# Down projection of a SwiGLU feed-forward block: from eight products of a two-by-two block to seven, in rounds between the gate and up products, for two of three token groups

## The chip, the cores and the metric

One core of one Trainium2 chip. The metric is device time in microseconds; before the change 2132.35 us is the median of three runs (2131.14 to 2133.75).

## The reference

One layer of a hybrid decoder on 2048 prompt tokens and 8 single-token samples (2056 columns in all, model width 1024): a normed input projection, a gated linear recurrence beside sliding-window attention, an output projection with residual, and then the part that matters here, all in float32:

```
hn = rmsnorm(h, norm2_g)
ff = silu(hn @ w_gate) * (hn @ w_up)        # w_gate, w_up: 1024 x 2816
y  = h + ff @ w_down                        # w_down: 2816 x 1024
y_out = rmsnorm(y, final_norm_g)
```

## The kernel before, in words

Every matrix product is done three times over, for precision: an operand is split into a high part, rounded to the engine's 32-bit replacement type (float32r), and a low part, the remainder; three matmuls (high x high, high x low, low x high) add up in one PSUM bank. ScalarE makes the high parts, the vector engine or GpSimd subtracts to get the low parts.

The feed-forward block (from about 700 us on) works through three groups of tokens (HALVES, L34: two halves of 344, then 342 columns each). In a group it goes through the 22 chunks of 128 hidden features as 11 pairs. For each pair, gate and up are each a two-by-two block product (two hidden chunks, two token halves, two halves of the model width) done Strassen-Winograd-wise: seven products (PRODS, L35) of four 128-deep pieces each, 7 x 4 x 3 = 84 matmuls. `products` (L1043) issues them, sums them from PSUM into tiles c (L1069 to L1102), applies silu on ScalarE (L1061), multiplies up by gate on GpSimd (L1064) and splits the result into fh and fl (L1066, L1067). `down` (L1105) takes the pair's 2 x 2 tiles of ff and the two rows of w_down: for each of eight output chunks m and two token halves n it does six matmuls into a bank (L1120 to L1122), and the vector engine adds the bank to the residual y in SBUF (L1124): 96 matmuls and 16 reads per pair.

The down projection of pair p stands between the gate and the up products of pair p + 1; that of the last pair stands at the group's end, with the first three gate products of the next group ahead of it (N_EARLY).

The weights of w_gate and w_up need sums for the seven products. In the first group these are built, split and stored to DRAM (split_s, four of seven a pair, L1033); the later groups load them (L1017), L_SS = 11 us ahead of use, and split the three plain ones (L986, L987). Weights of w_down are loaded (L1039) and split in each group, their low part on GpSimd (L1041). Split weights lie in a ring of eight tiles (wp and wp2), raw ones in a ring of seven.

A ring of sixteen big tiles (bigp) holds three slots of 344 columns in each tile: eight tiles for the activations of products 1, 2 and 6 (`hn_load`), six for the residual y (`y_load`, L982), so fourteen a group; tiles are handed out in turn, and a new owner waits for the old one. `hn_mix` prepares the next group's activations while a group runs (loads L322, scaling L326 and sums L334 on the vector engine, stores L330). `finish` (L1128) does the final norm of a group and stores it (L1148, L1151), inside the next group's first pairs.

PSUM has eight banks in five pools: acc has three, s two, t, o and m one each; the products and the down tiles take them in turn (`ps_tile`).

The order of the work is written out as times: each generator yields the time in a nominal schedule (U_M = 1.76 us a product, U_D = 14.1 us a down projection) at which its next step is due, and that time is the priority with which a scheduling pass, which simulates the program, orders each engine's queue. Every engine works its queue in order. All loads and stores here are issued by the sync engine's queue.

```
T_B = [T_B0 + i * (NPAIR * U_P + D_TB) for i in range(3)]
def t_gate(gi, p):
    return T_B[gi] + (2 * U_G + (p - 1) * U_P if p else 0)
def t_down(gi, p):
    return t_gate(gi, p + 1) + U_G if p < NPAIR - 1 else ...
```

Of the kernel before, what the change touches and what calls it, by code (L numbers as in the profile page):

```python
# [42 lines left out]
T_FS = 12.0  # L43
L_SS, L_ST = 11.0, 5.0
D_TB = 0.0
# [7 lines left out]
T_H3, D_H3 = T_B0 + 38, 4.0  # L53
T_B = [T_B0 + i * (NPAIR * U_P + D_TB) for i in range(3)]
O_KF = [8, 9, 10, 11, 12, 13, 0, 4, 1, 5, 2, 6, 3, 7]
# [89 lines left out]
def hybrid_step(tc, xT, xR, vecs, cst, gatew, win, wout, wgate, wup, wdown, kT, vC, ck, cv, sconv, sh0,  # L145
# [4 lines left out]
    with ExitStack() as ctx:  # L150
# [779 lines left out]
        with ExitStack() as bctx:  # L930
# [10 lines left out]
            def turn(key, n):  # L941
                cnt[key] += 1
                return cnt[key] % n
# [16 lines left out]

            ys, ws, gss, ffs = {}, {}, {}, {}

            def t_gate(gi, p):
                return T_B[gi] + (2 * U_G + (p - 1) * U_P if p else 0)

            def t_up(gi, p):
                return t_gate(gi, p) + U_G + (U_D if p else 0)

            def t_down(gi, p):
                return t_gate(gi, p + 1) + U_G if p < NPAIR - 1 else t_up(gi, p) + U_G + (N_EARLY * U_M if gi < len(HALVES) - 1 else 0)  # L970

            def t_prod(gi, p, x, i):
                t = t_gate(gi, p) if x == "g" else t_up(gi, p)
                return t + U_M * i - (U_D if gi and not p and x == "g" and i < N_EARLY else 0)

# [18 lines left out]
            def mixed_weights(src, gi, p, x):  # L994
# [17 lines left out]
                for i, r in enumerate(PRODS):  # L1012
# [18 lines left out]
                    if r in SPLIT:  # L1031
                        with at(tr - L_ST if p else tr + 2):
                            nc.sync.dma_start(split_s[x][p, SPLIT.index(r)], w.bitcast(F32))  # L1033

            def down_weights(gi, p, t):
                for i, (q, h) in enumerate(((0, 0), (0, 1), (1, 0), (1, 1))):
                    yield t + U_D / 4 * i - 16
                    v = raw_tile(f"rd{gi}_{p}_{h}{q}")
                    nc.sync.dma_start(v, wdown[2 * p + h][:, q * 512:q * 512 + 512])  # L1039
                    yield t + U_D / 4 * i - 9  # L1040
                    keep_weights(("d", gi, p, h, q), f"d{gi}_{p}_{h}{q}", v, nc.gpsimd)  # L1041

            def products(gi, p, x):  # L1043
# [3 lines left out]
                if up:  # L1047
                    fh = {(h, n): fp.tile([P, TP], F32R, tag=f"fh{h}{n}", name=f"fh{gi}_{p}_{h}{n}")
                          for h in range(2) for n in range(2)}
                    fl = {(h, n): fp.tile([P, TP], F32R, tag=f"fl{h}{n}", name=f"fl{gi}_{p}_{h}{n}")  # L1050
                          for h in range(2) for n in range(2)}
                    ffs[gi, p] = fh, fl
# [3 lines left out]
                c11, c12, c21, c22 = (C[h, n][:, :nn] for h in range(2) for n in range(2))  # L1056

                def finished(h, n):
# [5 lines left out]
                    (nc.vector if DVE_MUL == 1 or DVE_MUL == 2 and p == NPAIR - 1 else nc.gpsimd).tensor_tensor(v, v, g, op=ALU.mult)  # L1064
                    hi, lo = fh[h, n][:, :nn], fl[h, n][:, :nn]
                    nc.scalar.copy(hi, v)  # L1066
                    nc.vector.tensor_tensor(lo, v, hi.bitcast(F32), ALU.subtract)  # L1067

# [36 lines left out]
            def down(gi, p):  # L1105
                t = t_down(gi, p)
                last = p == NPAIR - 1
                yield t, ("udone", gi, p)
                fh, fl = ffs.pop((gi, p))
                nn = HALVES[gi][0][1]  # L1110
                order = [(m, n) for n in range(2) for m in range(KD)] if last else \
                    [(m, n) for m in range(KD) for n in range(2)]
                for i, (m, n) in enumerate(order):
                    yield t + U_D * i / 16, ("d", gi, p, 0, m // 4), ("d", gi, p, 1, m // 4)
                    ps = ps_tile(f"pd{gi}_{p}_{m}_{n}")[:, :nn]
                    for h in range(2):
                        w = ws["d", gi, p, h, m // 4]
                        c = m % 4 * P
                        hi, lo = fh[h, n][:, :nn], fl[h, n][:, :nn]
                        nc.tensor.matmul(ps, w[:, 0, c:c + P], hi, start=h == 0, stop=False)  # L1120
# [50 lines left out]
            for gi in range(len(HALVES)):  # L1171
# [6 lines left out]
                for n in range(2):  # L1178
                    te = tb + NPAIR * U_P
                    ch.add(finish(gi, n, te + 6 + 8 * n, 1.0) if gi < 2 else finish(gi, n, te + U_D * (n / 2 - 1) + 1, 0.8))  # L1180
                for p in range(NPAIR):
                    ch.add(mixed_weights(wgate, gi, p, "g"))
                    ch.add(mixed_weights(wup, gi, p, "u"))
                    ch.add(down_weights(gi, p, t_down(gi, p)))
                    ch.add(products(gi, p, "g"))
                    ch.add(products(gi, p, "u"))
                    ch.add(down(gi, p))
            ch.run()
# [101 lines left out]
```

## Time and profile before

| | |
|---|---|
| median of three runs | 2132.35 us |
| the profiled execution, its own time | 2133.11 us |
| its span, first to last instruction | 2131.3 us |
| mean granted TensorE clock | 0.989 |
| TensorE busy | 2057.4 us, 97% |
| vector engine busy | 1346.7 us, 63% |
| ScalarE busy | 838.2 us, 39% |
| GpSimd busy | 863.4 us, 41% |

Times in the rows count from the span's start. PE is TensorE's matmuls, DVE the vector engine, ACT ScalarE, POOL GpSimd, SP the sync engine's queue. A matmul's row is longer than its distance to the next one, since matmuls are pipelined. L12 is line 12 of the kernel. A wait is put down to what ended it.

### The profile page before, as it was taken

How to read it: one execution, taken by the hardware profiler on the slowest of the kernel's cores; microseconds unless marked ns; L12 is line 12 of the kernel's file. 1: busy time of each engine (PE TensorE's matmuls, PEld its weight loads, DVE VectorE, ACT ScalarE, POOL GpSimd, SP SyncE). 2: the span in 40 equal slices, each digit the busy share in tenths (PEclk: the TensorE clock that was granted, in tenths of full speed). 3: DMA queues.
4: the chain of work that ended last, by engine and by line, in shares of the span. 5: the costliest groups of instructions: out<-in, count | busy, mean ns of one | idle time of the engine just before them, and what ended most of it. 6: DMA issues, size and time to landing. Idle time of an engine off the chain costs nothing.

```text
span 2131.3 us, 34656 instructions
## 1 busy us (share of the span) xinstructions
PE 2057.4 (97%) x12454; PEld 1947.2 (91%) x12454; DVE 1346.7 (63%) x2551; ACT 838.2 (39%) x1714; POOL 863.4 (41%) x748
## 2 busy tenths in 40 slices
PE   8999899999999899999999999999999999999997
PEld 8887687878877899999999999999999999999997
DVE  6767974766985857767766655555546644444445
ACT  5746773563653443333234422222224322212222
POOL 5211342020122687677666523442344433323422
PEclk9999899999999999999999999999999999999998
DMA  8764394575678866665656575656557655545442
GB/s 303 251 214 139 117 305 157 169 254 188 214 247 264 305 205 210 207 210 201 213 185 219 193 245 193 206 179 211 188 167 239 204 197 180 169 158 167 163 156 73
DMA packets 188395, 429.72 MB, mean 202 GB/s; under 512 B 23072, under 2 KB 64432, under 8 KB 188208
## 3 DMA queue, kind: packets, MB, share of 16 engines
q1 hardware_dynamic: 185024, 424.99, 59.8%
q10 hardware_dynamic: 3200, 2.51, 0.4%
q8 instruction: 99, 1.62, 0.3%
q14 instruction: 72, 0.59, 0.1%
HBM read 326.46 MB, written 102.04 MB: 201 GB/s over the span
## 4 chain that ended last, share of the span: by engine, by line
PE 74%; DVE 10%; DMA 8%; ACT 3%; issue 3%; POOL 1%; SPq 0%; DVEq 0%; ACTq 0%; POOLq 0%
PE pd L1120 7%; PE pd L1121 7%; PE pd L1122 7%; PE ps_u L1082 6%; PE ps_u L1080 6%; PE ps_u L1081 6%; PE ps_g L1082 6%; PE ps_g L1081 6%; PE ps_g L1080 6%; PE ip L234 3%; PE ip L235 3%; PE ip L236 3%; DMA n<-hs 2%; DMA xs<-in_xT 1%; PE op L235 1%
## 5 line engine op out<-in xcount | busy, mean ns | idle before, releaser
L1124 DVE TENSOR_TENSOR y<-y,pd 128x342 f32<-128x342 f32 (+1 forms) x528 | 259.9, 508 | 152.4 <-PE pd L1122 142.0
L1121 PE MATMUL pd<-fl,w_d 128*128 128x342 f32 (+1 forms) x1056 | 339.6, 322 | 4.3 <-DVE fl L1067 4.3
L1120 PE MATMUL pd<-fh,w_d 128*128 128x342 f32 (+1 forms) x1056 | 338.4, 322 | 5.3 <-ACT fh L1066 3.9
L1122 PE MATMUL pd<-fh,w_d 128*128 128x342 f32 (+1 forms) x1056 | 338.9, 322 | 0.6 <-POOL w_d L987 0.6
L1081 PE MATMUL ps_g<-hn,w_g 128*128 128x342 f32 (+1 forms) x924 | 295.3, 320 | 2.4 <-DVE hn L383 2.4
L1080 PE MATMUL ps_u<-hn,w_u 128*128 128x342 f32 (+1 forms) x924 | 295.3, 320 | 0.5 <-DVE c_g L1070 0.5
L1082 PE MATMUL ps_g<-hn,w_g 128*128 128x342 f32 (+1 forms) x924 | 295.2, 319 | 0.5 <-DVE w_g L987 0.5
L1082 PE MATMUL ps_u<-hn,w_u 128*128 128x342 f32 (+1 forms) x924 | 295.3, 320 | 0.0
L1080 PE MATMUL ps_g<-hn,w_g 128*128 128x342 f32 (+1 forms) x924 | 295.2, 320 | 0.0
L1081 PE MATMUL ps_u<-hn,w_u 128*128 128x342 f32 (+1 forms) x924 | 295.0, 319 | 0.0
L987 POOL TENSOR_TENSOR w_u<-ru,w_u 128x512 fp32r<-128x512 f32 x66 | 90.9, 1377 | 439.6 <-ACT w_u L986 436.6
L234 PE MATMUL ip<-xn,w_in 128*128 128x512 f32 (+1 forms) x560 | 198.8, 362 | 13.7 <-ACT xn L239 9.7
L986 ACT CAST w_u<-ru 128x512 fp32r<-128x512 f32 x99 | 60.8, 620 | 372.5 <-PE pd L1122 245.2
L1120 PEld LDWEIGHTS pd<-fh,w_d 128*128 128x128 f32 x1056 | 200.2, 190 | 7.1 <-ACT fh L1066 4.5
L1121 PEld LDWEIGHTS pd<-fl,w_d 128*128 128x128 f32 x1056 | 200.8, 190 | 4.9 <-DVE fl L1067 4.9
L1122 PEld LDWEIGHTS pd<-fh,w_d 128*128 128x128 f32 x1056 | 200.7, 190 | 0.7 <-POOL w_d L987 0.7
L235 PE MATMUL ip<-xn,w_in 128*128 128x512 f32 (+1 forms) x560 | 200.3, 361 | 0.5 <-DVE xn L240 0.5
L1070 DVE TENSOR_TENSOR c_u<-c_u,ps_u 128x342 f32<-128x342 f32 (+1 forms) x231 | 114.6, 508 | 132.3 <-PE ps_u L1082 131.5
L236 PE MATMUL ip<-xn,w_in 128*128 128x512 f32 (+1 forms) x560 | 198.0, 356 | 0.2 <-POOL w_in L225 0.2
L1064 POOL TENSOR_TENSOR c_u<-c_u,c_g 128x342 f32<-128x342 f32 (+1 forms) x120 | 124.0, 1035 | 168.3 <-DVE c_u L1070 167.2
L987 POOL TENSOR_TENSOR w_d<-rd,w_d 128x512 fp32r<-128x512 f32 x132 | 184.5, 1415 | 8.7 <-ACT w_d L986 7.6
L1070 DVE TENSOR_TENSOR c_g<-c_g,ps_g 128x342 f32<-128x342 f32 (+1 forms) x231 | 113.4, 506 | 103.7 <-PE ps_g L1082 102.1
(270 smaller groups left out, 4592.5 us busy)
## 6 DMA issues: line engine op xcount, KB each, us to landing
w_g<-split_g SPq DMA_DIRECT2D x88, 512.0 KB, 4.5
w_u<-split_u SPq DMA_DIRECT2D x88, 512.0 KB, 4.2
w_in<-split_w SPq DMA_DIRECT2D x84, 512.0 KB, 3.4
rd<-in_wdown SPq DMA_DIRECT2D x132, 256.0 KB, 3.1
rg<-in_wgate SPq DMA_DIRECT2D x110, 256.0 KB, 3.0
ru<-in_wup SPq DMA_DIRECT2D x110, 256.0 KB, 3.1
w_out<-split_w SPq DMA_DIRECT2D x48, 512.0 KB, 5.2
split_g<-w_g SPq DMA_DIRECT2D x44, 512.0 KB, 3.0
```

The costliest lines, as they stand in the source:

```text
L234: nc.tensor.matmul(out, wh, xh, start=first, stop=False)
L235: nc.tensor.matmul(out, wh, xl, start=False, stop=False)
L236: nc.tensor.matmul(out, wl, xh, start=False, stop=last)
L987: lo_eng.tensor_tensor(w[:, 1, :], src, w[:, 0, :].bitcast(F32), op=ALU.subtract)
L1070: nc.vector.tensor_tensor(o, a, b, op)
L1080: nc.tensor.matmul(ps, wh, hi, start=kk == 0, stop=False)
L1081: nc.tensor.matmul(ps, wh, lo, start=False, stop=False)
L1082: nc.tensor.matmul(ps, wl, hi, start=False, stop=kk == 3)
L1120: nc.tensor.matmul(ps, w[:, 0, c:c + P], hi, start=h == 0, stop=False)
L1121: nc.tensor.matmul(ps, w[:, 0, c:c + P], lo, start=False, stop=False)
L1122: nc.tensor.matmul(ps, w[:, 1, c:c + P], hi, start=False, stop=h == 1)
L1124: nc.vector.tensor_tensor(ys[gi, n, m], ys[gi, n, m], ps, ALU.add)
```

## The change

In the second and third token group the down projection of pairs 1 to 9 is done with seven products of the two-by-two block (two hidden chunks, two token halves, two halves of the 1024 output columns) instead of eight. For each of two quarters of the output columns there are seven rounds, in the order DPRODS, and each round does two 128-wide tiles of three matmuls: 14 rounds, 84 matmuls a pair. A bank of key X collects products 1, 6, 7 and 4 one after the other, and one of key Z products 5 and 3; after each product the vector engine adds the bank's sum so far to one part of y, and later matmuls go on adding into the same bank: 28 reads a pair.

The rounds no longer stand between gate and up: from the third gate product of the next pair on, two rounds follow each product until all fourteen are done (T_ROUND, R_AT = 2). In these steps the gate and up products take only the acc banks. Three further combinations of the ff tiles and one that replaces the tile (0,1) are made on GpSimd and split; the three live in six slots of two more big tiles (`extra`), so that a group takes sixteen tiles of sixteen.

In the second group (`down_make`) w_down is loaded in pieces of 256 columns, four combinations for each of the two quarters are made on GpSimd, seven 512-column weight tiles are split (the low part of tiles 2 and 5 on GpSimd, of the five others on the vector engine) and stored to DRAM (split_d); in the third group (`down_load`) they are loaded from there. The lead L_SS of stored weights goes from 11 to 9 us. Pairs 0 and 10 and the first group keep the old `down`.

```diff
-L_SS, L_ST = 11.0, 5.0
+L_SS, L_ST = 9.0, 5.0
...
+DPRODS = [1, 5, 6, 3, 7, 2, 4]
+U_R, R_AT = 0.88, 2
+L_DR, L_DS, D_LO_POOL = 18.0, 10.5, (2, 5)
...
+def wino(gi, p):
+    return gi > 0 and 0 < p < NPAIR - 1
...
+def plan():
...
+            mixed = p and wino(gi, p - 1)
+            n = 0
+            for i in range(14):
+                if i == 7 and p and not mixed:
+                    down[gi, p - 1] = t
+                    t += U_D
+                prod[gi, p, "gu"[i // 7], i % 7] = t - (U_D if gi and not p and i < N_EARLY else 0)
+                t += U_M
+                if mixed and i >= R_AT:
+                    for n in range(n, min(14, n + 2)):
+                        rounds[gi, p - 1, n] = t
+                        t += U_R
+                    n += 1
...
+        split_d = dp.tile([NPAIR, 7, P, 2, 2, 256], F32, name="split_d")
...
+            def down_make(gi, p):
...
+                def quad(v, r, half):
+                    h, q = {1: (0, 0), 2: (1, 0), 4: (1, 1), 0: (0, 1)}[r]
+                    c = q * 512 + half * 256
+                    nc.sync.dma_start(v, wdown[2 * p + h][:, c:c + 256])
+                    A[r, half] = v
+
+                def load(j):
+                    v = pre[j] = raw_tile(f"rd{gi}_{p}_{j}").rearrange("p (a c) -> p a c", a=2)
+                    for n in (0, 1):
+                        i = 2 * j + n
+                        if j == 7:
+                            quad(v[:, n], 0, n)
+                        elif DPRODS[i % 7] in (1, 2, 4):
+                            quad(v[:, n], DPRODS[i % 7], i // 7)
+
+                def combine(n, half):
+                    r = DPRODS[n % 7]
+                    A11, A12, A21, A22 = (A[q, half] for q in (1, 2, 0, 4))
+                    a, b, op = {5: (A21, A22, ALU.add), 7: (A11, A21, ALU.subtract),
+                                6: (S.get(5), A11, ALU.subtract), 3: (A12, S.get(6), ALU.subtract)}[r]
+                    S[r] = pre[n // 2][:, n % 2]
+                    nc.gpsimd.tensor_tensor(S[r], a, b, op=op)
+
+                for j in range(7):
+                    t = T_ROUND[gi, p, 2 * j]
+                    for i in {0: (0, 7, 3, 2), 4: (6,)}.get(j, ()):
+                        yield t - L_DR
+                        load(i)
+                    yield t - L_DS
+                    if j not in pre:
+                        pre[j] = sum_tile(f"sd{p}_{j}").rearrange("p (a c) -> p a c", a=2)
+                    for n in (2 * j, 2 * j + 1):
+                        if DPRODS[n % 7] not in (1, 2, 4):
+                            combine(n, n // 7)
+                    yield t - L_DS + 1.5
+                    w = whl_tile(f"wd{gi}_{p}_{j}").rearrange("p a (b c) -> p a b c", b=2)
+                    nc.scalar.copy(w[:, :, 0], pre[j])
+                    (nc.gpsimd if j in D_LO_POOL else nc.vector).tensor_tensor(
+                        w[:, :, 1], pre[j], w[:, :, 0].bitcast(F32), op=ALU.subtract)
+                    ws["d", gi, p, j] = w
+                    fire(("d", gi, p, j))
+                    with at(t - 4):
+                        nc.sync.dma_start(split_d[p, j], w.bitcast(F32))
+
+            def down_load(gi, p):
+                for j in range(7):
+                    yield T_ROUND[gi, p, 2 * j] - L_SS
+                    w = whl_tile(f"wd{gi}_{p}_{j}").rearrange("p a (b c) -> p a b c", b=2)
+                    nc.sync.dma_start(w.bitcast(F32), split_d[p, j])
+                    ws["d", gi, p, j] = w
+                    fire(("d", gi, p, j))
...
+                combine = up and wino(gi, p)
+                if combine and gi not in extra:
+                    place = slots(bigp, "big", f"t{gi}", F32R)
+                    extra[gi] = [next(place) for _ in range(6)]
...
+                    if not combine:
+                        part((h, n), v, (fh[h, n], fl[h, n]))
+                    elif (h, n) != (0, 1):
+                        part({(0, 0): 1, (1, 0): 2, (1, 1): 3}[h, n], v, (fh[h, n], fl[h, n]))
+                    if combine and (h, n) == (0, 1):
+                        nc.gpsimd.tensor_tensor(c11, c12, c11, op=ALU.subtract)
+                        part(5, c11, (fh[0, 1], fl[0, 1]))
+                    elif combine and (h, n) == (1, 0):
+                        nc.gpsimd.tensor_tensor(c12, c22, c12, op=ALU.subtract)
+                        nc.gpsimd.tensor_tensor(c22, c22, c11, op=ALU.subtract)
+                        part(6, c22, extra[gi][0:2])
+                        part(7, c12, extra[gi][2:4])
+                        nc.gpsimd.tensor_tensor(c21, c21, c22, op=ALU.subtract)
...
-                    ps = ps_tile(f"ps_{name}_{r}")[:, :nn]
+                    ps = (acc_tile if p and wino(gi, p - 1) and R_AT <= i + 7 * up <= R_AT + 7 else ps_tile)(f"ps_{name}_{r}")[:, :nn]
...
+            BANKS = {(0, "X"): (s_tile, s_tile), (0, "Z"): (o_tile, t_tile), (0, 2): (m_tile, o_tile),
+                     (1, "X"): (t_tile, m_tile), (1, "Z"): (s_tile, s_tile), (1, 2): (o_tile, s_tile)}
+
+            def down_parts(gi, p):
+                nn = HALVES[gi][0][1]
+                acc = {}
+                for n in range(14):
+                    half, r = n // 7, DPRODS[n % 7]
+                    yield T_ROUND[gi, p, n], ("d", gi, p, n // 2), ("T", gi, p, r)
+                    hi, lo = ts.pop((gi, p, r)) if half else ts[gi, p, r]
+                    w = ws["d", gi, p, n // 2][:, n % 2]
+                    key = {1: "X", 6: "X", 7: "X", 4: "X", 5: "Z", 3: "Z", 2: 2}[r]
+                    fresh = r in (1, 5, 2)
+                    for j in range(2):
+                        m = 2 * half + j
+                        if fresh:
+                            acc[key, j] = BANKS[half, key][j](f"pw{gi}_{p}_{r}_{m}")[:, :nn]
+                        ps = acc[key, j]
+                        c = j * P
+                        nc.tensor.matmul(ps, w[:, 0, c:c + P], hi, start=fresh, stop=False, skip_group_check=not fresh)
+                        nc.tensor.matmul(ps, w[:, 0, c:c + P], lo, start=False, stop=False, skip_group_check=not fresh)
+                        nc.tensor.matmul(ps, w[:, 1, c:c + P], hi, start=False, stop=True, skip_group_check=not fresh)
+                        with ahead(4):
+                            for y in {1: (11,), 2: (11,), 6: (12,), 3: (12,), 7: (22,), 5: (22,), 4: (21,)}[r]:
+                                v = ys[gi, y % 10 - 1, m + (y // 10 - 1) * 4]
+                                nc.vector.tensor_tensor(v, v, ps, ALU.add)
 
...
-                    ch.add(down_weights(gi, p, t_down(gi, p)))
+                    ch.add((down_load if gi == 2 else down_make)(gi, p) if wino(gi, p) else down_weights(gi, p, T_DOWN[gi, p]))
+                    ch.add((down_parts if wino(gi, p) else down)(gi, p))
```

## Rows read from the trace of the kernel before

**Rows 1.** The page of the profile: busy time, share of the span and count of instructions of each engine, and TensorE's granted clock in 40 equal slices (tenths of full speed).

```profile
PE 2057.4 (97%) x12454; PEld 1947.2 (91%) x12454; DVE 1346.7 (63%) x2551; ACT 838.2 (39%) x1714; POOL 863.4 (41%) x748
PEclk9999899999999999999999999999999999999998
```

**Rows 2.** Busy time by stretch (view of windows): stretch, its length, busy us and instructions of PE, PEld, DVE, ACT and POOL, granted clock, busy share of the DMA engines, GB/s. Steady pairs of the second group, of the third, and of the first.

```profile
1261.00:1594.00 333.00, 333.00 (x2118) 333.00 (x2117) 174.82 (x323) 83.19 (x165) 120.20 (x98) 1.00 0.58 190
1716.00:2008.00 292.00, 292.00 (x1855) 292.00 (x1854) 131.65 (x253) 71.76 (x140) 102.37 (x85) 1.00 0.50 165
1050.00:1100.00 50.00, 50.00 (x319) 50.00 (x318) 34.06 (x57) 17.65 (x34) 37.17 (x29) 1.00 0.58 206
```

**Rows 3.** The end of the second group: the same view of windows; then TensorE's instructions in order of time (start, us, in brackets the idle time before and what ended it); then, from the chain of waits, the first and the last but one of a run of matmuls at this distance (start, us to the next).

```profile
1640.00:1645.00 5.00, 2.62 (x10) 2.33 (x11) 5.00 (x8) 3.01 (x8) 2.92 (x3) 0.73 1.03 376
1645.00:1650.00 5.00, 5.00 (x22) 5.00 (x22) 3.55 (x9) 2.94 (x7) 3.08 (x3) 0.59 1.00 360
...
1640.50 0.58 PE L1120 MATMUL pd<-fh,w_d 128*128 128x342 f32 x2 [2.30 <-ACT fh L1066]
1643.12 0.65 PE L1121 MATMUL pd<-fl,w_d 128*128 128x342 f32 x1 [1.88 <-DVE fl L1067]
...
1644.35 0.28 PE pd L1120
...
1648.91 0.28 PE pd L1121
```

**Rows 4.** Groups of instructions by line, engine and operation, 1261 to 1594 us (eight pairs of the second group): shape, count, busy us, mean ns of one, idle before. The last two rows are of the views of one tile and of one line: duration in ns, least, median and longest.

```profile
L1124 DVE TENSOR_TENSOR y<-y,pd 128x342 f32<-128x342 f32 x128 | 64.4, 510 | 43.5 <-PE pd L1122 43.2
L1067 DVE TENSOR_TENSOR fl<-c_u,fh 128x342 fp32r<-128x342 f32 x33 | 25.0, 758 | 11.8 <-ACT fh L1066 11.7
L326 DVE SCALAR_TENSOR_TENSOR n<-n,vec,hb 128x342 f32<-128x342 f32 x16 | 12.3, 766 | 19.2 <-DMA n<-hs 19.2
L987 DVE TENSOR_TENSOR w_u<-ru,w_u 128x512 fp32r<-128x512 f32 x8 | 6.0, 745 | 0.0
L987 POOL TENSOR_TENSOR w_d<-rd,w_d 128x512 fp32r<-128x512 f32 x33 | 46.1, 1418 | 3.0 <-ACT w_d L986 2.9
L1064 POOL TENSOR_TENSOR c_u<-c_u,c_g 128x342 f32<-128x342 f32 x32 | 33.2, 1037 | 61.2 <-DVE c_u L1070 61.2
L986 ACT CAST w_d<-rd 128x512 fp32r<-128x512 f32 x33 | 20.4, 618 | 4.3 <-PE ps_g L1082 4.3
L1066 ACT CAST fh<-c_u 128x342 fp32r<-128x342 f32 x33 | 15.8, 480 | 71.6 <-POOL c_u L1064 71.6
...
L1124 DVE TENSOR_TENSOR y<-y,pd x528: 495/511/515, 758.4 to 2115.2; 128x342 f32<-128x342 f32 x117, 128x344 f32<-128x344 f32 x59
...
L1067 DVE TENSOR_TENSOR fl<-c_u,fh x33: 506/609/1601, 1261.4 to 1593.8; 128x342 fp32r<-128x342 f32 x33
```

**Rows 5.** Order of time around one read of a down tile: TensorE's instructions, then the vector engine's (start, us).

```profile
1313.46 0.32 PE L1122 MATMUL pd<-fh,w_d 128*128 128x342 f32 x1
1313.62 0.32 PE L1120 MATMUL pd<-fh,w_d 128*128 128x342 f32 x1
...
1313.81 0.51 DVE L1124 TENSOR_TENSOR y<-y,pd 128x342 f32<-128x342 f32 x1
```

**Rows 6.** Who waited for whom, vector engine, 1261 to 1594 us: us in total, times, longest us.

```profile
DVE n L326 <- DMA n<-hs: 19.2, 15, 2.6
DVE w_g L987 <- ACT w_g L986: 15.4, 6, 3.6
DVE fl L1067 <- ACT fh L1066: 11.7, 9, 1.8
```

**Rows 7.** DMA of two stretches, 1261 to 1594 us and 1150 to 1180 us (the change from the first to the second group): packets, MB and mean GB/s; a queue's packets, MB and share of the 16 engines; one line's issues, KB each, median us to landing.

```profile
DMA packets 27594, 63.23 MB, mean 190 GB/s; under 512 B 3070, under 2 KB 9086, under 8 KB 27567
w_g<-split_g SPq DMA_DIRECT2D x32, 512.0 KB, 4.6
...
DMA packets 5969, 9.31 MB, mean 310 GB/s; under 512 B 658, under 2 KB 4551, under 8 KB 5966
q1 hardware_dynamic: 5966, 9.27, 91.8%
w_g<-split_g SPq DMA_DIRECT2D x4, 512.0 KB, 5.8
```

**Rows 8.** Order of time at the start of the third group: the sync queue's issues, TensorE's first matmul of its first down projection, and the vector engine.

```profile
1641.64 4.89 SPq L982 DMA_DIRECT2D y<-hs  x6
...
1697.95 1.90 SPq L1151 DMA_DIRECT2D out_yT<-y  x4
1701.77 0.33 SPq L982 DMA_DIRECT2D y<-hs  x1
...
1694.12 0.32 PE L1120 MATMUL pd<-fh,w_d 128*128 128x342 f32 x1
...
1695.26 0.51 DVE L1124 TENSOR_TENSOR y<-y,pd 128x342 f32<-128x342 f32 x1 [0.24 <-PE pd L1122]
...
1701.24 1.35 DVE L1124 TENSOR_TENSOR y<-y,pd 128x342 f32<-128x342 f32 x3
1702.51 0.92 DVE L1070 TENSOR_TENSOR c_g<-c_g,ps_g 128x342 f32<-128x342 f32 x2
1704.71 0.51 DVE L1124 TENSOR_TENSOR y<-y,pd 128x342 f32<-128x342 f32 x1 [1.28 <-DMA y<-hs]
```

More of the change, by code (lines that the diff above doesn't have):

```diff
@@ L53 @@
 T_H3, D_H3 = T_B0 + 38, 4.0
-T_B = [T_B0 + i * (NPAIR * U_P + D_TB) for i in range(3)]
+DPRODS = [1, 5, 6, 3, 7, 2, 4]
[4 more added lines that the diff above has]
+def plan():
+    t, begin, end, prod, down, rounds = T_B0, [], [], {}, {}, {}
+    for gi in range(len(HALVES)):
+        begin.append(t)
+        for p in range(NPAIR):
+            mixed = p and wino(gi, p - 1)
[11 more added lines that the diff above has]
+                    n += 1
+        down[gi, p] = t + (N_EARLY * U_M if gi < len(HALVES) - 1 else 0)
+        t += U_D
+        end.append(t)
+    return begin, end, prod, down, rounds
+T_B, T_END, T_PROD, T_DOWN, T_ROUND = plan()
 O_KF = [8, 9, 10, 11, 12, 13, 0, 4, 1, 5, 2, 6, 3, 7]
@@ L959, in ps_tile @@
                 return (acc_tile, s_tile, o_tile, acc_tile, s_tile, t_tile, acc_tile, m_tile)[turn("ps", 8)](name)
[L961 to L970, printed above, removed]
+            ys, ws, gss, ts, extra = {}, {}, {}, {}, {}
             def t_prod(gi, p, x, i):
-                t = t_gate(gi, p) if x == "g" else t_up(gi, p)
-                return t + U_M * i - (U_D if gi and not p and x == "g" and i < N_EARLY else 0)
+                return T_PROD[gi, p, x, i]
             def y_load(gi, t):
@@ L1033, in mixed_weights, with sum_tile @@
                             nc.sync.dma_start(split_s[x][p, SPLIT.index(r)], w.bitcast(F32))
+            def sum_tile(name):
+                pool, tag = (sqp, "sq") if turn("sq", 4) < 2 else (bcp, "bc")
+                return pool.tile([P, TM], F32, tag=tag, name=name)[:, :512]
             def down_weights(gi, p, t):
@@ L1056, in products, with part @@
                 c11, c12, c21, c22 = (C[h, n][:, :nn] for h in range(2) for n in range(2))
+                combine = up and wino(gi, p)
+                if combine and gi not in extra:
+                    place = slots(bigp, "big", f"t{gi}", F32R)
+                    extra[gi] = [next(place) for _ in range(6)]
+                def part(r, v, place):
+                    hi, lo = (x[:, :nn] for x in place)
+                    nc.scalar.copy(hi, v)
+                    nc.vector.tensor_tensor(lo, v, hi.bitcast(F32), ALU.subtract)
+                    ts[gi, p, r] = hi, lo
+                    fire(("T", gi, p, r))
                 def finished(h, n):
@@ L1064, in finished @@
                     (nc.vector if DVE_MUL == 1 or DVE_MUL == 2 and p == NPAIR - 1 else nc.gpsimd).tensor_tensor(v, v, g, op=ALU.mult)
-                    hi, lo = fh[h, n][:, :nn], fl[h, n][:, :nn]
-                    nc.scalar.copy(hi, v)
-                    nc.vector.tensor_tensor(lo, v, hi.bitcast(F32), ALU.subtract)
+                    if not combine:
[11 more added lines that the diff above has]
+                        nc.gpsimd.tensor_tensor(c21, c21, c22, op=ALU.subtract)
+                        part(4, c21, extra[gi][4:6])
                 def add(o, a, b, op=ALU.add):
@@ L1183, in hybrid_step @@
                     ch.add(mixed_weights(wup, gi, p, "u"))
-                    ch.add(down_weights(gi, p, t_down(gi, p)))
+                    ch.add((down_load if gi == 2 else down_make)(gi, p) if wino(gi, p) else down_weights(gi, p, T_DOWN[gi, p]))
                     ch.add(products(gi, p, "g"))
                     ch.add(products(gi, p, "u"))
-                    ch.add(down(gi, p))
+                    ch.add((down_parts if wino(gi, p) else down)(gi, p))
             ch.run()
```

9 lines of the change are left out of this document (4 added, 5 removed).

## The prediction

> **What bounds the kernel now.** I read the page first: TensorE is busy for 97% of the span at full granted clock, the vector engine for 63% [rows 1]. An average hides stages, so next the busy time by stretch: in the steady pairs of the second group (1261 to 1594) and of the third (1716 to 2008) TensorE has no idle microsecond, the vector engine is at 52% and 45%, GpSimd at 36% and 35%, the DMA engines at 0.58 and 0.50 [rows 2]. 2118 matmuls in 333.00 us are 0.157 us each, so a pair (2 x 7 x 12 + 96 = 264 matmuls) takes 41.5 us. Here only fewer matmuls make the program shorter. Idle TensorE appears between groups: 2.30 and 1.88 us before 1643, after which the granted clock reads 0.73 and 0.59 and twenty matmuls follow each other in 0.29 us, the lower of its two levels [rows 3].
>
> **What is removed.** For pairs 1 to 9 the down projection goes from 16 x 6 = 96 matmuls to 14 rounds of 2 x 3 = 84. That is 12 x 9 x 2 = 216 matmuls fewer, of the same shape, x 0.157 = **34.0 us**, all on the path. A pair would take 39.6 us.
>
> **What is added on the vector engine.** Reads of PSUM rise from 16 to 28 a pair: 12 x 0.510 = 6.1 us. Three more parts need their low halves: 3 x 0.758 = 2.3 us. In the second group five of the seven new weight tiles get their low half here: 5 x 0.745 = 3.7 us [rows 4]. The second group so goes from 0.525 x 41.5 = 21.8 to 33.9 us of 39.6 (86%), the third, whose weights come finished from DRAM, from 18.7 to 27 (68%).
>
> Most of it falls into the mixed stretch, seven steps of 12 + 12 matmuls (3.77 us each, 26.4 in all): 28 x 0.51 reads, 7 x 0.51 adds of the gate and up products, about 4 x 0.76 for low halves, 4 x 0.745 for weights, and 2 of the next group's norm mixing at 0.77, some 25 us of 26.4. Instructions overlap a little (three reads in a row take 1.35 us [rows 8], not 1.53), so it fits, barely.
>
> The SBUF-only subtraction runs from 0.506 to 1.601 us while the PSUM read never leaves 0.495 to 0.515 [rows 4], so something delays only the former. The Trainium skill (SBUF — State Buffer, Who interferes with whom) says that a vector instruction with two SBUF inputs and a GpSimd instruction that reads SBUF exclude each other for a whole instruction, while one with at most one SBUF input is untouched; the spread agrees. By row means the addition is 12.1 us a pair; by the rule at its worst each of the eight would wait for a whole GpSimd instruction. I take the means and keep the worst for a rival.
>
> **The new waits.** A bank that held product 1 is read by the vector engine and then accumulated into two rounds later; TensorE's queue is in order, so a late read holds the next gate products too. In the trace a tile's last matmul starts at 1313.46, the next begins at 1313.62, and the read ends at 1314.32 [rows 5]: 0.70 us after the issue. The first tile of a round is therefore free 0.47 + 0.70 = 1.2 us after the round begins and wanted after 3.77: slack 2.6 us with an idle vector engine. The same engine waits up to 2.6 us for the norm loads, 3.6 for a weight cast and 1.8 for the high half of a part [rows 6]. With queued reads behind them some of these reach TensorE. Second group: 8 pairs hold 15 norm waits, so 9 have some 17, two thirds in the mixed stretch, 11. Lowest cost 0; highest, when each comes on top of a slow subtraction and a denser DMA queue, 2.6 + 1.6 + 1.2 - 2.6 = 2.8 us, 31 us. Most waits are half their maximum (19.2 / 15 = 1.3 us), which the slack covers, so I go near the low end: 0.55 us each, **6 us**. Third group: no norm mixing, longest waits under the slack; 0 to 9 x (1.8 + 1.6 - 2.6) = 7 us, I take **1.5**.
>
> **What I cost at nothing, and its cover.** GpSimd in the second group: two weight halves instead of four (-2 x 1.418), eight new 256-wide combinations (not in the trace; between 0.71, half of the 512-wide row, and 1.04, the 342-wide row: I take 0.85), four part combinations at 1.037: 15.0 + 8.1 = 23 us of 39.6 [rows 4]. ScalarE gains 3 x 0.618 + 3 x 0.480 = 3.3 us on 10.4. The longest part chain after the last up product (add 0.51, three GpSimd instructions, copy 0.48, subtraction 0.76) takes 4.9 us, and its first user comes three gate products, two rounds and another product later, 9.4 us. If that cover goes, round 3 is late. In the mixed stretch gate products have three banks only, but come every 3.77 us: 11 us to read one.
>
> **DMA.** Second group: 63.23 MB in 333 us is 7.9 MB a pair; seven stores of 0.524 MB make it 11.55 MB in 39.6 us, 292 GB/s. At 310 GB/s (1150 to 1180) the engines are 92% busy and 512 KB weight loads land in 5.8 us instead of 4.6 [rows 7]. The lead of the stored gate and up weights is cut from 11 to 9 us, leaving 3 us over 5.8, and a sync queue that goes from 18 to 29 issues a pair, about 0.4 us each. Stores of the new weights wait in that queue for their low halves, and later loads wait behind them. I cost this at 0: the 2.8 us above already contains the 1.2 us of slower landing. The third group comes to 6.9 - 1.05 + 3.67 = 9.5 MB a pair, 239 GB/s, well below.
>
> **The change of groups.** Two tiles of the big ring now hold part combinations, so every group takes 16 of 16 instead of 14. Before, the third group's residual could load six of its sixteen pieces at 1641, into tiles of the old activations; the next load came at 1701.77, after the final scaling and store had freed a tile, and the vector engine still waited for a load at 1704.71 [rows 8]. Afterwards all six tiles follow the second group's output one for one, so the first down read falls at 1704.7 instead of 1695.26. TensorE begins that projection at 1694.12 and can fill six to eight banks at 0.94 us (one or two still hold gate sums): it stops at 1699.8 to 1701.7 and resumes at 1705.2, an idle of 3.5 to 5.4 us. Lowest 0 (if earlier work fills it), highest 5.4 + 2.6 us for 20 matmuls at the lower clock, as [rows 3] show behind the other idle: I take **5**. The third group's first activations also lose two early tiles; they were loaded when those behind them came free, so 0.5 us (0 to 2).
>
> **Sum:** 34.0 - 6 - 1.5 - 5 - 0.5 = 21.0. The profiled execution took 2133.11, so 2112.1; it stands 0.76 above the median, hence **2111.3 us**.
>
> **Rivals.** First, every cover holds: only the change of groups costs (0 to 5), 2099 to 2104. For it: the first group runs at 68% vector, 74% GpSimd and 0.58 DMA load with TensorE full [rows 2]. Against: there no matmul waits for a read so soon.
>
> Second, the vector engine is full in the second group. Each of eight new SBUF-only instructions waits for a whole GpSimd one, 8 x 1.037 less the 0.8 us by which the mean of the three subtractions stands above their minimum already, 7.5 more: 33.9 + 7.5 = 41.4 us a pair. That group then keeps its 41.5 us, and the sum is 17 - 5 - 0.5 - 1.5 = 10, so 2122; with part of the engine's time overlapped it is 2118, with some of its own waits on top 2131. The exclusion in that rule is what would do it; against it speaks that the mean stays at 0.758.
>
> Third, on the other side: the reads are late in every pair and the clock follows. Two idles of 2.30 and 1.88 us were followed by matmuls 0.29 apart, 20 of them, 2.6 us lost [rows 3]. One such event in each of 18 pairs costs 18 x (4.2 + 2.6) = 122 us; it decides from 34.0 - 5.5 = 28.5 us, that is from five such events, or at 0.23 us of waiting in each of the 126 steps without any. Five to eight events give 2138 to 2158. The Trainium skill (TensorE: Matmul & The Clock Gate, A second HAM failure mode: psum-queue depth-cycling) reports a kernel whose short idles between PSUM groups kept the clock swinging. Against: the slack of 2.6 us, and that the steady windows hold 1.00.
>
> **How the numbers follow.** Forecast (2104 to 2118) 0.55; every cover holds 0.18; vector engine full (2118 to 2131) 0.15; slower 0.12. A measurement can tell 0.2%, 4.3 us: faster is below 2128, slower above 2136.6. Faster: 0.55 + 0.18 + 0.09 = 0.82; same 0.06; slower 0.12. The range takes in the first three cases: 2098 to 2131, about 0.85 of the chance.
>
> **What would show it.** Right: 12238 matmuls, vector engine near 86% and 68% in the two groups' steady stretches, a few short TensorE waits on reads of the new tiles, mostly in the second group, and one of 3 to 5 us at the third group's first down projection behind the residual's load. Wrong: TensorE waiting for weight tiles (the DMA or the sync queue then decides), the granted clock below 1.00 inside steady pairs, or no wait at all.

## The result, and the profile after

The changed kernel took 2113.1 us in the median of four runs (2107.43 to 2114.69), the kernel before 2131.74 us (2130.18 to 2133.75): a ratio of 0.9907, 95% interval 0.9886 to 0.9929. The forecast was 2111.3 us in a range of 2098 to 2131. So the total came out 1.8 us from the forecast; the sections below show that its terms did not.

The page, of the execution that took 2114.55 us (span 2112.8); its rows answer to [rows 1].

```profile
PE 2032.7 (96%) x12238; PEld 1916.2 (91%) x12238; DVE 1532.0 (73%) x2866; ACT 860.0 (41%) x1759; POOL 931.5 (44%) x838
PEclk9999899999999999999999999999999999999998
```

216 matmuls are gone, as counted, and the vector engine has 185 us more work. The same stretches as in [rows 2]: the second group's steady pairs, then the third's.

```profile
1250.00:1610.00 360.00, 349.12 (x2178) 343.38 (x2179) 288.86 (x512) 116.54 (x227) 200.31 (x191) 1.00 0.80 277
1720.00:2040.00 320.00, 320.00 (x2039) 320.00 (x2038) 216.25 (x411) 75.93 (x152) 106.55 (x97) 1.00 0.68 240
```

The third group is what the forecast described: 2039 matmuls in 320.00 us, 0.157 each, no idle time, the vector engine at 68%. The second is not: at 0.157 the 2178 matmuls take 342 us of its 360. What its vector engine does there and what it waits for, as in [rows 4] and [rows 6]:

```profile
L1256 DVE TENSOR_TENSOR y<-y,pw 128x342 f32<-128x342 f32 x228 | 106.7, 502 | 8.9 <-PE pw L1252 8.1
L1147 DVE TENSOR_TENSOR fl<-c_u,fh 128x342 fp32r<-128x342 f32 x36 | 33.3, 925 | 15.8 <-ACT fh L1146 15.6
L1147 DVE TENSOR_TENSOR t<-c_u,t 128x342 fp32r<-128x342 f32 x27 | 29.7, 1110 | 1.2 <-ACT t L1146 1.1
...
L360 DVE SCALAR_TENSOR_TENSOR n<-n,vec,hb 128x342 f32<-128x342 f32 x16 | 11.8, 736 | 25.2 <-DMA n<-hs 25.2
...
DVE n L360 <- DMA n<-hs: 25.2, 9, 4.5
DVE fl L1147 <- ACT fh L1146: 15.6, 17, 2.3
```

The PSUM read costs what it did (0.502 us). Subtractions that read SBUF alone cost more than the 0.758 of before: 0.925 and 1.110 us, with GpSimd now busy 56% of the stretch. That agrees with the Trainium skill (SBUF — State Buffer, Who interferes with whom), by which a vector instruction with two SBUF inputs and a GpSimd instruction that reads SBUF shut each other out; the read of a bank that goes on adding up has one of its inputs in PSUM. But the price does not simply follow GpSimd's busy share: in a run below with GpSimd at 72% the same two rows show 0.899 and 0.889 us. What TensorE waited for in the second group (1185 to 1638), and the DMA rows that answer to [rows 7]:

```profile
PE ps_u L1184 <- DMA w_u<-split_u: 5.8, 4, 3.0
PE pw L1250 <- DVE y L1256: 1.3, 3, 0.7
...
PE pw L1251 <- DVE t L1147: 0.9, 1, 0.9
PE ps_u L1184 <- DVE y L1256: 0.6, 1, 0.6
```

```profile
DMA packets 42696, 99.61 MB, mean 277 GB/s; under 512 B 4747, under 2 KB 19240, under 8 KB 42664
q1 hardware_dynamic: 42664, 99.21, 79.5%
split_d<-wd SPq DMA_DIRECT2D x60, 512.0 KB, 4.5
w_u<-split_u SPq DMA_DIRECT2D x33, 512.0 KB, 6.1
```

These waits count only time in which no matmul was in flight. To see all of it, I took the starts of neighbouring feed-forward matmuls and added up what is over 0.157 us (where over 0.03). Called **gaps** below, they come to 1.2 us in the second group of the kernel before and 19.0 in the changed one (from 22 us after the group's start on), to 0.3 and 0.7 in the third. Each is put down to what ended the idle time; a gap whose row names none (about 6 us) is a wait shorter than a matmul's overlap, or one of a run at the lower clock.

The account of the profiled executions, from the start of the last up matmul of one group to that of the next:

| stretch, us | before | changed | difference |
|---|---|---|---|
| to the first up matmul | 716.7 | 719.9 | +3.2 |
| first group | 446.6 | 447.3 | +0.7 |
| second group | 468.4 | 471.1 | +2.7 |
| third group, with the change of groups before it | 467.5 | 442.8 | -24.7 |
| from there to the end | 32.0 | 31.7 | -0.4 |

The sum is -18.5 us, the difference of the spans. In each of the last two groups 108 matmuls are missing, 17.0 us. Nine gate matmuls of the third group, 1.4 us, now start before the second's last up matmul (1635.19 to 1636.60) and so stand in the second's stretch. **The second group lost all of its gain again; the third kept it, and the change of groups gave another 6.3.** The first 3.9 us are not the change: in both traces every engine's instructions come in the same order up to there. They are the difference of two executions: in ten of the runs below that have this same order, the first two stretches took 716.1 to 721.3 and 446.5 to 452.1 us.

How late weights stop TensorE: in order of time the sync queue, TensorE's next up product, and the stretch after it.

```profile
1404.88 0.33 SPq L1116 DMA_DIRECT2D split_d<-wd  x1
1405.26 0.45 SPq L1077 DMA_DIRECT2D rd<-in_wdown  x1
1405.81 0.74 SPq L1041 DMA_DIRECT2D w_u<-split_u  x1
1407.59 0.81 SPq L1077 DMA_DIRECT2D rd<-in_wdown  x2
1408.50 0.86 SPq L1041 DMA_DIRECT2D w_u<-split_u  x2
...
1408.97 0.38 SPq L1041 DMA_DIRECT2D w_u<-split_u  x1
...
1415.65 0.42 PE L1184 MATMUL ps_u<-hn,w_u 128*128 128x342 f32 x1 [3.01 <-DMA w_u<-split_u]
...
1415.00:1420.00 5.00, 4.35 (x18) 4.35 (x19) 3.10 (x7) 0.00 (x0) 0.00 (x0) 0.66 0.51 173
```

Line 1041 loads stored gate and up weights. In 1404 to 1409 they stand among a store of a new weight tile and loads of w_down (the row at 1408.50 holds two, the second of them shown again by itself). The one that TensorE waits for, by its semaphore, is issued at 1408.97, only 3.7 us before TensorE is ready for it at 1412.64, where the lead is 9 us; it lands 6.6 us later, and TensorE goes on at 1415.65, 3.01 us late. After that the granted clock is 0.66 and 18 matmuls take 4.35 us, 1.5 us more than at the full level. It is the one such event in the second group's steady pairs; the rest ran at 1.00.

The change of groups, to set against [rows 3] and [rows 8]: TensorE's idle time and the clock after it, the residual's loads, and the first and the fourth group of reads of the third group's first down projection.

```profile
1645.89 0.59 PE L1223 MATMUL pd<-fh,w_d 128*128 128x342 f32 x2 [1.74 <-ACT fh L1146]
...
1645.00:1650.00 5.00, 4.11 (x26) 4.11 (x27) 3.92 (x8) 4.27 (x11) 2.48 (x2) 1.00 1.00 300
...
1631.28 0.42 SPq L1006 DMA_DIRECT2D y<-hs  x1
1635.50 0.32 SPq L1006 DMA_DIRECT2D y<-hs  x1
...
1636.23 0.79 SPq L1006 DMA_DIRECT2D y<-hs  x2
...
1648.57 1.97 SPq L1006 DMA_DIRECT2D y<-hs  x2
...
1701.73 0.33 SPq L1006 DMA_DIRECT2D y<-hs  x1
...
1695.23 0.50 DVE L1227 TENSOR_TENSOR y<-y,pd 128x342 f32<-128x342 f32 x1
...
1704.33 0.51 DVE L1227 TENSOR_TENSOR y<-y,pd 128x342 f32<-128x342 f32 x1 [1.22 <-DMA y<-hs]
```

Before: two idles, 4.2 us, and a spell at half clock. Now: one of 1.74 us, and the clock stays at 1.00. And six loads of the residual still come by 1650.5, where the forecast had none before 1701.

### The profile page after: what moved, and what is told of

It reads as the page before. It is cut to its first block, busy times and chain, and to the rows that moved or that the text cites. A ratio compares the mean times of both kernels' runs of the same rounds, so it can differ in the third digit from the quotient of the medians.

```text
span 2112.8 us, 34962 instructions
## 1 busy us (share of the span) xinstructions
PE 2032.7 (96%) x12238; PEld 1916.2 (91%) x12238; DVE 1532.0 (73%) x2866; ACT 860.0 (41%) x1759; POOL 931.5 (44%) x838
## 4 chain that ended last, share of the span: by engine, by line
PE 38%; DMA 5%; DVE 5%; POOL 2%; issue 2%; SPq 1%; ACT 0%; DVEq 0%; POOLq 0%; ACTq 0%
PE ps_u L1184 4%; PE ps_u L1186 4%; PE ps_u L1185 4%; PE ps_g L1184 4%; PE ps_g L1186 4%; PE ps_g L1185 4%; PE pw L1251 3%; PE pw L1250 3%; PE pw L1252 3%; PE pd L1223 2%; PE pd L1224 2%; PE pd L1225 2%; DMA rd<-in_wdown 1%; DMA n<-hs 1%; DMA w_u<-split_u 1%
## 5 line engine op out<-in xcount | busy, mean ns | idle before, releaser
L1256 DVE TENSOR_TENSOR y<-y,pw 128x342 f32<-128x342 f32 x504 | 240.4, 505 | 60.8 <-PE pw L1252 58.1
L1184 PEld LDWEIGHTS ps_u<-hn,w_u 128*128 128x128 f32 x924 | 174.3, 189 | 9.4 <-DMA w_u<-split_u 6.2
L1185 PEld LDWEIGHTS ps_g<-hn,w_g 128*128 128x128 f32 x924 | 174.1, 188 | 2.9 <-DVE hn L417 2.9
L1184 PEld LDWEIGHTS ps_g<-hn,w_g 128*128 128x128 f32 x924 | 174.1, 188 | 0.8 <-issue 0.6
L1186 PEld LDWEIGHTS ps_g<-hn,w_g 128*128 128x128 f32 x924 | 174.1, 188 | 0.8 <-DVE w_g L1011 0.8
L1185 PEld LDWEIGHTS ps_u<-hn,w_u 128*128 128x128 f32 x924 | 174.5, 189 | 0.0
L1186 PEld LDWEIGHTS ps_u<-hn,w_u 128*128 128x128 f32 x924 | 174.2, 189 | 0.1
L1223 PE MATMUL pd<-fh,w_d 128*128 128x344 f32 (+1 forms) x480 | 153.7, 324 | 5.7 <-ACT fh L1146 3.4
L1147 DVE TENSOR_TENSOR fl<-c_u,fh 128x342 fp32r<-128x342 f32 (+1 forms) x132 | 118.5, 898 | 53.7 <-ACT fh L1146 53.4
L1224 PE MATMUL pd<-fl,w_d 128*128 128x344 f32 (+1 forms) x480 | 154.7, 323 | 2.4 <-DVE fl L1147 2.4
```

Of the source, the lines that this page charges most:

```text
L1184: nc.tensor.matmul(ps, wh, hi, start=kk == 0, stop=False)
L1185: nc.tensor.matmul(ps, wh, lo, start=False, stop=False)
L1186: nc.tensor.matmul(ps, wl, hi, start=False, stop=kk == 3)
L1224: nc.tensor.matmul(ps, w[:, 0, c:c + P], lo, start=False, stop=False)
L1256: nc.vector.tensor_tensor(v, v, ps, ALU.add)
```

## The experiments

The ratios are to the kernel before, run beside each kernel on its chip. **Theory A**: in the second group stored weights land late, for the sync queue, the traffic of the new stores, or the shorter lead. **Theory B**: the vector engine there is full, or blocked, so its reads and low halves are late.

**Each group by itself.** Second group alone:

```diff
-    return gi > 0 and 0 < p < NPAIR - 1
+    return gi == 1 and 0 < p < NPAIR - 1
```

> Rounds in the second group alone (stores included, nobody loads them); the third group keeps the old down projection. From the traces the second group gains nothing: the stretch between the last up matmul of one group and of the next went from 468.4 to 471.1 us, the third from 467.5 to 442.8, of which some 17 us are the removed matmuls and the rest the change of groups. Expected with all theories: 2126 to 2134, second stretch 469 to 473; below 2122 would say that the second group does gain.

Ratio 0.9965 (0.9950 to 0.9981), median 2127.09 us. Its second stretch is 467.2 us, just under the expected 469, with gaps of 19.2, of which 5.9 wait for w_u. Third group alone (`gi == 2`, `down_make` without its store):

> Rounds in the third group alone, with weights made there and not stored; the second group keeps the old down projection. No norm mixing and no stores run in the third group. Theory A: gaps under 5 us in the third group, its stretch 448 to 455, total 2112 to 2119. Theory B, the vector engine's added work by itself: gaps of 8 us or more, total 2121 or more.

Ratio 0.9938 (0.9919 to 0.9956), median 2124.95 us; gaps 5.4 in the third group, just over A's bound and under B's, its stretch 455.4, at A's end, but the median lies in B's range (2121 or more), in a set of runs in which the kernel before took 2137.1: neither theory is met in full. The two ratios multiply to 0.9903, the whole change gave 0.9907: two thirds of the gain are the third group's. Where the second group alone gains its 0.35% stays open: its profile is of an execution of 2134.05 us, 7 us above its median.

**Without the detour through DRAM.**

```diff
-                    with at(t - 4):
-                        nc.sync.dma_start(split_d[p, j], w.bitcast(F32))
...
-                    ch.add((down_load if gi == 2 else down_make)(gi, p) if wino(gi, p) else ...
+                    ch.add(down_make(gi, p) if wino(gi, p) else ...
```

> The third group makes its own down weights as the second does, and no group stores them (split_d is not used). In the changed kernel the second group has 19.1 us of gaps between its matmuls (1185 to 1640 us), the third 0.7. Theory A (the weight path: stores that wait in the sync queue, and their traffic, make the stored gate and up weights land late): the second group's gaps fall under 9 us, the third's stay under 6, total 2100 to 2108. Theory B (the vector engine is full: late reads and late low halves): the second group keeps over 14 us, the third gets 6 to 15, total 2113 to 2125.

Ratio 0.9900 (0.9882 to 0.9918). Windows of the second and the third group, the vector engine's longest wait in the second, and TensorE's: in the second for w_u, in the third all.

```profile
1250.00:1610.00 360.00, 351.13 (x2197) 344.54 (x2197) 286.15 (x516) 117.62 (x231) 202.56 (x194) 1.00 0.59 190
1720.00:2040.00 320.00, 319.81 (x2035) 319.32 (x2034) 246.98 (x451) 109.53 (x211) 181.33 (x178) 1.00 0.53 173
...
DVE n L360 <- DMA n<-hs: 32.8, 13, 6.9
...
PE ps_u L1182 <- DMA w_u<-split_u: 0.8, 1, 0.8
...
PE pd L1221 <- DVE y L1225: 1.4, 1, 1.4
PE pw L1248 <- DVE y L1254: 0.2, 1, 0.2
```

The DMA engines fall from 0.80 to 0.59 and the waits for w_u from 5.8 to 0.8 us. Gaps: 15.4 in the second group, 2.6 in the third. So the stores cost some 4 us of gaps (those that wait for w_u fall by 5.5, others grow by 2), and B's bound for the second group holds, but not for the third: there the same rounds, making the same weights on a vector engine at 77%, run almost freely. GpSimd's waits for w_down are alike in both (62 and 66 us in all), so they are not the reason either. What the second group has and the third has not is the mixing of the next group's norm: 32 vector instructions that wait 33 us for their loads, 16 loads and 28 stores. That it is this mixing is argued from what is left over; no run leaves it out.

**Blocked by the norm's loads?** First a later due time for the scaling, `ahead(-6 if gi else 0)` for `ahead(0)` at line 359:

> In the second and third group's norm mixing the scaling on the vector engine is due 6 us after its load instead of at once; work and traffic are the same. In the changed kernel the vector engine stands still for 25 us in the second group (9 waits, up to 4.5) behind such loads. Theory B (the vector engine, blocked and full): these waits fall under 8 us, gaps between matmuls of the second group from 19 to 9 to 14 us, total 2104 to 2110 against 2113. Theory A (the weight path): gaps stay over 16 us, total within 3 us of 2113.

```profile
DVE n L360 <- DMA n<-hs: 22.5, 9, 4.5
```

Ratio 0.9913 (0.9893 to 0.9933), gaps 21.3. The wait did not go away, so nothing was tested: every engine's instructions came out in the same order as in the changed kernel. This is that kernel once more, and shows how far two profiles of equal queues differ: gaps of 19.0 and 21.3 us, of which 6.5 and 5.7 wait for w_u. Differences of some 2 us of gaps say nothing. Then loads issued half a step or a whole one before their scaling (the loop of `hn_mix` rewritten, `fetch` one `yield` ahead of `scale`):

```diff
+                    yield t0 + dt * 2 / 8
+                    make(kk, 7, x, n22, x, ALU.subtract)
+                    n11 = fetch(kk, 0, 0)
+                    yield t0 + dt * 3 / 8
+                    scale(kk, 0, 0, n11)
```

> The changed kernel with the norm mixing's loads really issued earlier: each 4 to 8 us before its scaling's step (the run with a later due time left the waits at 22.5 us, so it tested nothing). Theory B (the vector engine's queue blocked by these loads): its waits for n fall from 25 to under 6 us and the gaps of the second group by 4 to 9 us, ratio to the kernel before 0.986 to 0.989. If the blocked time was only spare time of the vector engine: gaps stay at 17 to 21 us, ratio 0.990 to 0.992.

```profile
DVE n L359 <- DMA n<-hs: 15.8, 9, 3.6
...
PE ps_u L1234 <- DMA w_u<-split_u: 8.2, 5, 3.2
PE pw L1300 <- DVE y L1306: 2.2, 2, 1.4
```

Ratio 0.9948 (0.9932 to 0.9964), slower than the change. The waits fell by 9 us only, not to 6, and the gaps did not fall (23.7, 9.0 of them for w_u); the first group, which mixes too, took 454.4 us instead of 447.3. Fewer microseconds of waiting on the vector engine bought nothing: this form of theory B fails, and what in the norm mixing costs the second group stays open.

**Stores later, or from another queue.** `at(t + 1)` for `at(t - 4)`:

> Only the due time of the split_d stores goes from 4 us before to 1 us after the round, so that the low halves are done when the sync queue comes to a store; the traffic is the same. If waiting stores hold up the loads behind them (theory A, its queue part): gaps of the second group from 19 to 8 to 13 us, total 2102 to 2108. If it is the traffic (theory A, its DMA part) or the vector engine (theory B): 17 us or more, total within 3 us of 2113.

```profile
PE ps_u L1184 <- DMA w_u<-split_u: 8.7, 4, 3.6
```

Ratio 0.9919 (0.9888 to 0.9950), gaps 23.2: not the stores' waiting in the queue. With `nc.scalar.dma_start`:

> The stores of split_d are issued from ScalarE's queue instead of the sync engine's; the traffic is the same. Theory A, its queue part: the waits for w_u fall under 3 us, total 2106 to 2111. If the traffic is what makes them late: 5 us or more stay. ScalarE then waits for the low halves (up to 3.4 us each as the sync queue did), which may hold up silu and the high halves: in that case waits for fh and t grow and the total is 2113 or more.

```profile
PE ps_u L1184 <- DMA w_u<-split_u: 8.8, 5, 3.2
PE pw L1250 <- DVE y L1256: 4.4, 5, 1.3
```

Ratio 0.9951 (0.9933 to 0.9968), gaps 30.3: out of the sync queue's way the stores left the w_u waits as long as ever, and more reads were late. So it is not the stores' own wait in that queue. The queue still delays the loads: in this run the load behind the longest wait, 3.2 us, stood behind loads of w_down of which the first was issued at 1406.33, 2.0 us after the instruction before it was through. What both runs leave of the stores is their traffic.

**Less on the vector engine.**

```diff
-L_DR, L_DS, D_LO_POOL = 18.0, 10.5, (2, 5)
+L_DR, L_DS, D_LO_POOL = 18.0, 10.5, (0, 1, 2, 3, 4, 5, 6)
```

> The low halves of all seven new weight tiles of the second group go to GpSimd instead of two of them: 5 x 0.9 = 4.5 us a pair less on the vector engine, 5 x 1.4 = 7 us more on GpSimd (from 56% to about 73%). Theory B: gaps from 19 to 11 to 15 us, total 2106 to 2111. If the exclusion between the two engines or GpSimd's longer chain eats it: 17 us or more, total 2112 to 2120. Theory A: the stores come later (GpSimd takes 1.4 us), the waits for w_u grow over 6.5 us.

```profile
1250.00:1610.00 360.00, 352.81 (x2219) 348.26 (x2218) 258.36 (x475) 120.59 (x234) 260.64 (x240) 1.00 0.81 279
...
PE ps_u L1184 <- DMA w_u<-split_u: 2.7, 4, 1.1
PE pw L1250 <- DVE y L1256: 2.5, 5, 0.7
```

Ratio 0.9875 (0.9860 to 0.9890). The vector engine goes from 80% to 72%, GpSimd to 72%, gaps to 14.2, inside B's bounds. The gaps that waited for low halves, 1.9, are gone; those for w_u fell too, from 6.5 to 3.4, against A's forecast; those for reads into y are no shorter (5.8, against 3.6 and, in the second profile of the changed kernel, 5.7).

**The lead.**

```diff
-L_SS, L_ST = 9.0, 5.0
+L_SS, L_ST = 11.0, 5.0
```

> The lead of stored weights goes back from 9 to 11 us, for gate and up of both groups and for the third group's down weights. Theory A, if the lead is what lacks: the waits for w_u of 6.5 us fall under 3, gaps from 19 to about 14, total 2107 to 2111. If the ring of eight tiles or the sync queue sets the time of issue: no change within 3 us, or slower, since the sync queue then waits for tiles longer.

```profile
PE pw L1250 <- DVE y L1256: 1.6, 2, 1.4
PE ps_g L1184 <- DMA w_g<-split_g: 1.4, 1, 1.4
PE pw L1251 <- DVE t L1147: 1.4, 2, 1.1
PE ps_u L1184 <- DMA w_u<-split_u: 0.9, 1, 0.9
```

Ratio 0.9864 (0.9847 to 0.9880), 2105.6 us: the best version run, ahead of both kernels. Gaps 12.0, of which 1.1 for w_u, and a second stretch of 459.8 us against 471.1. With 13 us:

> The changed kernel with a lead of 13 us for stored weights (9 in the change, 11 in the kernel before). If a short lead was a cost by itself (theory A), the waits for w_u stay under 2 us, as with 11, gaps 10 to 14 us, ratio 0.985 to 0.988; more than 11 cannot help much, since the ring of eight tiles holds about 13 us of work. If the gain with 11 was one lucky order of the queues: gaps 16 us or more, ratio 0.990 or above.

```profile
PE pw L1250 <- DVE y L1256: 2.7, 4, 1.1
PE ps_g L1184 <- DVE c_g L1174: 2.6, 1, 2.6
PE ps_g L1184 <- DMA w_g<-split_g: 1.0, 2, 0.6
```

Ratio 0.9874 (0.9858 to 0.9891). No wait for w_u is left, which fits a lead that was too short; but gaps are 17.6, over the forecast's 14 and in the range set for a gain that was one lucky order of the queues, while the ratio lies in the other range. Most of the gaps with a name now wait for the vector engine.

**Together.** Lead 11 with all low halves on GpSimd, then with the earlier norm loads as well:

> The two edits that helped alone, together: lead of stored weights 11 us (gaps 12.0, ratio 0.9864) and all low halves of the new weights on GpSimd (gaps 14.2, 0.9875). If the late loads and the full vector engine are separate costs (theories A and B each hold for a part): gaps 6 to 9 us, ratio 0.983 to 0.985. If both worked on the same waits: 11 us or more, 0.986 or above.

> Lead 11, low halves on GpSimd, and the norm loads ahead of their use. If all three costs are separate: gaps under 6 us, ratio 0.981 to 0.984. If the norm loads cost nothing: as lead 11 with low halves on GpSimd, within 0.001.

```profile
PE ps_u L1184 <- DMA w_u<-split_u: 3.0, 5, 1.2
```

Ratios 0.9904 (0.9880 to 0.9929) and 0.9944 (0.9923 to 0.9965), gaps 14.5 and 19.2, w_u waits of 3.8 (the row shows their idle time) and 6.0. Two edits that help alone do not add up, and both forecasts of separate costs, 6 to 9 us and under 6, missed. With the same lead of 11 us the waits for w_u are back, so the lead alone does not decide them. The first kernel's four runs lie at 2107.75 and 2114.58 to 2115.81; its profile is of the shortest. Each edit of a due time or an engine lets the scheduling pass order all queues anew, so an edit's effect here is its own plus that of another order; I did not separate the two.

## Why the prediction was right, and where it was not

**What bounds it, and the 34.0 us.** Right. The third group's steady pairs show it undisturbed: no idle, 0.157 us a matmul, so 17.0 us for its 108.

**The vector engine's added work.** Foreseen as 86% and 68%, measured 80% and 68%; GpSimd foreseen as 58%, measured 56%. The work itself was foreseen well, 33.9 us a pair against 33.4; its share is lower because a pair takes 41.7 us and not 39.6. That the third group runs free fits the slack of 2.6 us for a read of a bank that goes on adding up; its forecast 1.5 us was 0.4.

**The second group, 6 us.** Wrong in size and partly in kind: gaps rose by 17.8 us. The step that failed is the one on DMA, "I cost this at 0": the weight loads landed in 6.1 us, near the 5.8 assumed, but the 3 us left over did not cover the wait in the sync queue; the load behind the longest stop was issued 3.7 us ahead instead of 9. Waits for w_u are 6.5 us of the gaps (5.8 of idle time and the lost overlap of four matmuls). Without the stores they are 0.9; a lead of 11 us alone brought them to 1.1 and the kernel 0.4% down, though they came back with that lead and another edit. Of the other 12.5 us, 6.1 are put down to the vector engine (reads into y 3.6, low halves 1.9, a sum of an up product 0.6), 0.5 to w_g, and 6 have no name. These late reads and low halves are the kind of wait that the text had. Its main reason for them, a vector engine held up by the norm's loads, is not borne out: taking away part of these waits takes nothing off the gaps. Less work on the engine ended the waits for low halves but not those for reads.

**The change of groups, 5 us.** Wrong. The claim that all residual tiles follow the old output one for one fails at six loads by 1650.5; tiles were free for them as before (which ones, the traces do not tell), and the first read is at 1695.23, against 1695.26 before. The fourth group waits 1.22 us for its tile, as it did before, and TensorE waits for nothing between 1690 and 1730. The activations' 0.5 us was wrong in sign. There are 2.4 us less of idle and 2.6 us less at half clock. A likely reason, not tested: with the last rounds spread over the gate and up products of the last pair, 22.9 us instead of 17.7 lie between the start of the activations' loads (1619.84 in both) and the last down projection. Of the 6.3 us that the change of groups gave, 5 are these; the rest I have not placed.

**The sum.** 21.0 us forecast, 18.6 measured. Terms missed by 12 us for the worse (second group) and by 13 for the better (change of groups, third group), and 4 us lay between two executions of equal work. The total was right by luck: they cancelled. Two of the prediction's own signs of being wrong came: TensorE waited for weight tiles, and the granted clock fell once inside the steady pairs. Of its signs of being right, the wait of 3 to 5 us at the third group's first down projection did not come.

**The rivals.** "Every cover holds" is true of the third group alone. "The vector engine is full" described the second group's outcome, its whole gain gone, though by late weights as much as by that engine. The clock's swing, the rival on the slower side, came once, 1.5 us. The rule cited there, of short idles between PSUM groups that keep the clock swinging (the Trainium skill, TensorE: Matmul & The Clock Gate, A second HAM failure mode: psum-queue depth-cycling), did not decide: some fifteen idles under 1.6 us left the clock at 1.00.

**What stays open**: whether it is the norm mixing, and what in it, that makes the same rounds cost 13 us more of gaps in the second group than in the third; what the 6 us of gaps without a name wait for; and how much of each edit's effect is a new order of the queues.

## What to carry to other kernels

Removing work from the engine that bounds a stage pays only where the stage's other queues have room for what replaces it; look at each stage by itself, since here one group kept the whole gain and its twin none of it. When a change adds transfers, reckon the lead of the loads that are already there as time of issue plus landing under the new traffic, and do not shorten it in the same step. A total that fits proves little about its terms: lay the two traces side by side, stretch by stretch.

## What the runs showed of the hardware that was not expected

A matmul that had to wait costs more than its idle time says: start to start, the 3.01 us idle was 3.17 us late and the 0.30 us one 0.46, since the overlap of about 0.16 us with the one before is lost. Equal instruction queues took 716.7 and 719.9 us to the same matmul, two profiles of one order of all queues had 19.0 and 21.3 us of gaps, and medians of the kernel before lay between 2131.7 and 2137.1 us in different sets of runs, so under half a per cent only kernels that ran beside each other can be compared.
